# Fold behind the first pool tile, a third quad in the turns, split output weights kept in DRAM

## The chip, the cores and the metric

One Trainium2 chip, one of its cores. The metric is the time of one execution on the device in microseconds, as the median of several runs. Five engines run their own instruction queues: TensorE (PE), VectorE (DVE), ScalarE (ACT), GpSimd (POOL) and SyncE (SP). SP issues nearly all DMA transfers.

## The reference, cut to what matters

One decoder block on 2048 tokens of 1024 features, all float32:

```
z = rmsnorm(x) @ w_in + b_in              # 1024 -> 1536: a, gate, p of 512 each
conv = silu(layernorm(dwconv31(a * sigmoid(gate))))
pool_i = (trailing mean over w_i - p_i) @ w_pool[i], times s_pool   # 4 groups of 128, w = 2, 4, 8, 16
h = x + concat(conv, pool) @ w_out
h = h + (silu(hn @ w_gate) * (hn @ w_up)) @ w_down,  hn = rmsnorm(h)   # hidden width 2816
out = rmsnorm(h)
```

## The kernel before

**Products in float32.** Each operand of a large matmul is split into a high and a low part: ACT rounds it (`split`, L197), DVE subtracts (L198). `mm3` (L206 to L208) then issues three matmuls, high by high, high by low and low by high. A matmul has a 128x128 stationary block (weights) and 512 moving columns (tokens).

**Tiling.** The tokens go in two tiles of 1024 (`a0`, `a1`, `Sup`), each in two blocks of 512. Features lie on partitions. A tile passes the input projection (`in_tile`, with `in_evac` or `pool_evac`), the branches (`conv`, `ln`, `pool`), the output projection (`mix_out`, PSUM tile `px`), the norm (`norm`) and the feed-forward part (`gate_up`). The second tile's projection and branches run beside the first one's later stages.

**The fold.** The pool group's linear map is folded into the output weights: `fold()` splits `w_pool * s_pool`, and then, in four steps, loads 512 KB of `w_out`'s pool rows (`Dense(wop[i])`), splits them, issues 6 matmuls, copies the result and writes it to DRAM as `wf_d`. At the top level its first step stands behind the second GLU tile; the other four stand between the last two pairs of input tiles.

**Output weights.** `mix_out(b)` runs eight weight tiles for each block b, and is called for b = 0 and b = 1. `Ahead` makes each tile (two loads of 256 KB into staging, a split) two tiles ahead of its use, in both blocks and for both token tiles: 32 times in all.

**Quads.** Gate and up projections use one level of Strassen's scheme: a quad (L859 on) is 256 output features by 1024 tokens by 1024 inputs, in seven products of 12 matmuls instead of eight. Products 1 to 7 use token factors `t[1]` to `t[7]`, made by `put_t` from the four quarters of the normed h, and weight factors a to d made by `first` (a), `sums` (d, then four additions in place, L895 to L898), `mid` (b) and `last` (c). Quads with an even number are gates, the others ups. A quad's results lie in one PSUM tile of two halves (`acc`); the intermediate `ch` is one half of the PSUM tile `chain`, quads taking turns. Product 1 is copied from `acc` to `ch` (L971), and then product 2 adds to `acc`.

**The turn.** `turn(s, gu)` leads from the output projection to the quads. It steps three generators by hand: `m1` (`mix_out(1)`), `nm` (the norms; row sums L319, spread of the factors through a matmul with ones L349, scaling of eight columns L641) and `gu` (`gate_up`). In the transition `gate_up` runs quads 0 and 1 product by product while `put_t` makes the factors; the others follow in a loop, each quad's first product beside the end of the one before.

**What sets the order.** The order in which the kernel's text issues instructions gives priorities. A scheduler lays them out at compile time with its own estimate of times, per engine: the first ready one in the text's order goes first, so later work is drawn forward into gaps it foresees. On the chip each engine's order, SP's DMA queue too, is fixed. SBUF is given out by two lists of slots, `arena` (17 slots, staging and float32 data) and `arena_r` (36 slots, split data): `take` picks the free slot that was given back longest ago, in the text's order, and the new user waits for the old one's readers.

Of the kernel before, what the change touches and what calls it, by code (L numbers as in the profile page):

```python
# [104 lines left out]
def block_kernel(ctx: ExitStack, tc: tile.TileContext, x, xt, wi, wo, wop, wg, wu, wd, wp, par, out):  # L105
# [41 lines left out]
    p_d = dram("p_d", NCI, PH + TT)  # L147
    y_d = [dram(f"y_d{s}", KD, TT) for s in range(NS)]
    wf_d = dr.tile([P, KD * CC], F32, name="wf_d", bufs=1)
    h_d = [dram(f"h_d{s}", NQ, 2 * TT) for s in range(NS)]  # L150
# [59 lines left out]
    class Dense:  # L210


        def __init__(self, src, halves=False, parts=None, pairs=None):
            self.place = (lambda k: (k % pairs, k // pairs)) if pairs else (lambda k: (k // 2, k % 2))
            n = src.shape[1] // 2 if parts is None else T
            st = Buf(arena, 2 * n)
            v = st.ap.rearrange("p (a n) -> p a n", a=2)
            self.w = W(2, n)
            w = self.w.v
            self.per = n // P  # L220
            if halves:
                self.part = lambda a: (nc.sync.dma_start(v[:, a], src[:, a * n : (a + 1) * n]), split(w[:, 0, a], w[:, 1, a], v[:, a]))
                self.st = st
                return
            else:
                if parts is None:
                    nc.sync.dma_start(v, src.rearrange("p (a n) -> p a n", a=2))
                else:
                    parts(v)
                split(w[:, 0], w[:, 1], v)  # L230
            st.free()

# [122 lines left out]
    class Sup:  # L355
# [235 lines left out]
        def mix_weights(self):  # L591
            def maker(m):
                def parts(v):
                    nc.sync.dma_start(v[:, 0], wo[m])
                    nc.sync.dma_start(v[:, 1], wf_d[:, m * CC : (m + 1) * CC])

                return lambda: Dense(None, parts=parts)

            self.mw = Ahead([maker(m) for m in range(KD)] * 2, 2)
            self.mw.prime(2)  # L600

        def mix_out(self, b):
            self.hr = Rms(NT // 2)
            if b == 0:
                self.h = []
            ws = self.mw
            ks = list(range(NCI, KD)) + list(range(NCI))
            for q in range(NQ):
# [25 lines left out]
        def norm(self, b, hr, bank=None):  # L634

            hr.rows(1.0 / D, RMS_EPS, bank)
            yield
            hr.spread()
            for k in range(KD):
                v = self.h[k // 2].v[:, k % 2, b]  # L640
                stt(out=v, in0=v, scalar=col(O_GF, k), in1=hr.rb[:, 0], op0=ALU.mult, op1=ALU.mult)  # L641
                if k % 2:
                    yield
# [3 lines left out]
        def put_t(self, p, half, blk, *terms):  # L647

            self.t[p] = R(f"t{p}")
            for j in range(2):  # L650
# [7 lines left out]
        def gate_up(self):  # L658
# [13 lines left out]
            q0.load()  # L672
            q1.load()
            yield
            yield from self.put_t(1, *B11)
            yield from self.put_t(2, *B21)
            q0.first()
            q1.first()
            q0.sums()
            q0.mid()  # L680
            q1.sums()
            q0.begin()
            q1.begin()
            self.bank = q0.acc[:, 1]
            yield
            q0.product(1)
            yield
            q0.product(2)
            yield
            q1.product(1)  # L690
            q1.product(2)
            q1.mid()
            yield
            yield from self.put_t(5, *B11, B12, B11)
# [12 lines left out]
            run(self.put_t(4, *B21, B21, B11))  # L707
            quads[2].first()
            q0.product(4)
# [5 lines left out]
            quads[2].sums()  # L715
            quads[2].product(1)
            q1.product(4)
# [4 lines left out]
            for n in range(2, len(quads) - 2):  # L722
                cur, nxt, far = quads[n : n + 3]
                cur.product(2)
                cur.last()
                if far and n > 1:
                    far.load()
# [131 lines left out]
    class Quad:  # L859
# [6 lines left out]
        at = None  # L866
        acc = None

        def __init__(self, sup, n):
# [64 lines left out]
        def result(self, a, b, acc, extra=None):  # L934
# [6 lines left out]
            else:  # L941
                tt(out=dst, in0=acc, in1=dst, op=ALU.mult)

        def begin(self):
            if self.acc is None:
                self.acc = ps2("quad")

        def product(self, p):
            if p == 1:
                self.begin()  # L950
                self.open()
            b1, b5, ch = self.acc[:, 0], self.acc[:, 1], self.ch
# [17 lines left out]
            if p == 1:  # L970
                nc.scalar.copy(ch, b1)  # L971
            elif p == 2:
                self.result(0, 0, b1)
            elif p == 6:
# [125 lines left out]
    for i in range(2, NCI):  # L1100
        pa = a0.in_tile(in0.get(), "pa")
        step(cv, 5)
        step(fo)
        pg = a0.in_tile(in0.get(), "pg")
        a0.in_evac(i, pa, pg)
        step(cv, 4)
        step(fo)
    run(fo)
    sq1 = a1.squares()
    for i in range(NCI):  # L1110
        pp = a0.in_tile(in0.get(), "pp")
        a0.pool_evac(i, pp)
        step(cv, 4)
        if i < 3:
# [33 lines left out]
    def turn(s, gu):  # L1148
# [5 lines left out]
        step(m1)  # L1154
        step(nm)
        step(m1, 2)
        step(gu)
        for n, _ in enumerate(m1):
            if n < 2:
                step(nm, 2)  # L1160
            elif n == 2:
                step(nm)
            elif n < 5:
                step(gu, 2)
            elif n == 6:
                step(gu)
# [92 lines left out]
```

## Time and profile before

| | |
|---|---|
| Three runs | 1859.98, 1857.26, 1859.78 us; median 1859.78 |
| The profiled execution | 1857.97 us, span 1856.2 us |
| PE busy | 97%, 7803 matmuls |
| DVE busy | 75% |
| ACT busy | 38% |
| DMA, all queues | 289 MB, 156 GB/s over the span |
| Mean granted clock of PE | 0.988 |

The stages of the first token tile, from the timeline of PE: input projection to 155 us, with the fold's matmuls between 70 and 109; the second tile's input projection and the first one's convolution to 319; output projection to 410; transition to some 450; quads and the down projection after that. The second token tile's output projection runs from 1082 to 1171, its transition to some 1213.

A busy PE is not PE at its peak, since its matmuls overlap and their ends are modelled; the count of matmuls in a stretch says more. A line like L198 is that of a helper, so its groups hold many tiles.

### The profile page before, as it was taken

Reading aid. Unit: us, or ns where it says so; the run is one execution under the profiler, and the core shown is the slowest. Engines: PE = TensorE matmul, PEld = TensorE weight load, DVE = VectorE, ACT = ScalarE, POOL = GpSimd, SP = SyncE. Lnnn points to the kernel's source line nnn. Section 1 sums busy time; section 2 is a strip of 40 time slices with the busy share of each in tenths; the row PEclk is TensorE's granted clock in tenths of the full one; section 3 lists DMA queues with packets and bytes.
Section 4 is the critical chain, followed back from the end, with each engine's and each line's share of the span. In section 5 each row is a group of like instructions: output and inputs, shape, how many; then the busy total and the mean of one; then the engine's idle time right before and its main releaser. Section 6 shows DMA issues by size and latency. Waiting matters only on the chain.

```text
span 1856.2 us, 19925 instructions
## 1 busy us (share of the span) xinstructions
PE 1799.8 (97%) x7803; PEld 1460.2 (79%) x7803; DVE 1389.7 (75%) x1607; ACT 698.9 (38%) x900; POOL 54.1 (3%) x41
## 2 busy tenths in 40 slices
PE   8999999998999999999999999899999999999996
PEld 6887887876888888887778878678888888787885
DVE  5979997388899987999987546866555554868645
ACT  6255125234333333344444323333333333635420
POOL 0013200000000000000000000000000000000000
PEclk9999999999999999999999999999999999999998
DMA  8263224622343222337578763144423232667532
GB/s 301 75 210 125 69 92 159 223 84 91 131 166 113 97 97 98 130 109 275 207 271 303 260 207 114 68 175 156 151 87 146 86 108 91 231 245 272 215 103 91
DMA packets 84511, 289.15 MB, mean 156 GB/s; under 512 B 7616, under 2 KB 11840, under 8 KB 71104
## 3 DMA queue, kind: packets, MB, share of 16 engines
q1 hardware_dynamic: 83120, 285.69, 43.4%
q10 hardware_dynamic: 1296, 2.19, 0.3%
q8 instruction: 61, 1.00, 0.2%
q14 instruction: 34, 0.28, 0.0%
HBM read 201.77 MB, written 86.08 MB: 155 GB/s over the span
## 4 chain that ended last, share of the span: by engine, by line
PE 77%; DVE 10%; DMA 6%; ACT 3%; issue 2%; SPq 0%; POOL 0%; POOLq 0%; DVEq 0%; ACTq 0%
PE quad L206 10%; PE quad L207 10%; PE quad L208 10%; PE chain L206 8%; PE chain L207 8%; PE chain L208 8%; DVE arena_r L198 4%; PE px L206 2%; PE px L207 2%; PE px L208 2%; PE pd L206 2%; PE pd L208 2%; PE pd L207 2%; DVE arena L496 2%; ACT arena_r L197 1%
## 5 line engine op out<-in xcount | busy, mean ns | idle before, releaser
L197 ACT CAST arena_r<-arena 128x1024 fp32r<-128x1024 f32 (+2 forms) x431 | 414.6, 976 | 715.1 <-PE quad L207 199.1
L198 DVE TENSOR_TENSOR arena_r<-arena,arena_r 128x1024 fp32r<-128x1024 f32 (+2 forms) x431 | 479.9, 1129 | 181.1 <-ACT arena_r L197 176.7
L206 PE MATMUL quad<-arena_r 128*128 128x512 f32 x960 | 375.7, 392 | 4.3 <-ACT chain L971 1.4
L207 PE MATMUL quad<-arena_r 128*128 128x512 f32 x960 | 375.0, 391 | 1.3 <-DVE arena_r L198 1.3
L208 PE MATMUL quad<-arena_r 128*128 128x512 f32 x960 | 374.9, 391 | 0.0
L206 PE MATMUL chain<-arena_r 128*128 128x512 f32 x720 | 290.3, 403 | 12.0 <-ACT chain L971 6.6
L496 DVE SCALAR_TENSOR_TENSOR arena<-arena,par_sb 128x1024 f32<-128x1024 f32 (+1 forms) x240 | 287.5, 1214 | 2.5
L207 PE MATMUL chain<-arena_r 128*128 128x512 f32 x720 | 282.9, 393 | 5.2 <-DVE arena_r L198 5.2
L208 PE MATMUL chain<-arena_r 128*128 128x512 f32 x720 | 283.1, 393 | 0.0
L206 PEld LDWEIGHTS quad<-arena_r 128*128 128x128 f32 x960 | 180.8, 188 | 46.1 <-DVE arena L1010 2.8
L207 PEld LDWEIGHTS quad<-arena_r 128*128 128x128 f32 x960 | 181.0, 189 | 39.4 <-DVE arena_r L198 2.1
L208 PEld LDWEIGHTS quad<-arena_r 128*128 128x128 f32 x960 | 180.9, 188 | 37.8
L206 PEld LDWEIGHTS chain<-arena_r 128*128 128x128 f32 x720 | 136.2, 189 | 58.8 <-ACT chain L971 22.0
L207 PEld LDWEIGHTS chain<-arena_r 128*128 128x128 f32 x720 | 136.5, 190 | 33.9 <-DVE arena_r L198 6.7
L208 PEld LDWEIGHTS chain<-arena_r 128*128 128x128 f32 x720 | 136.3, 189 | 29.7
L206 PE MATMUL px<-arena_r 128*128 128x512 f32 x256 | 100.1, 392 | 1.0 <-DVE arena L622 1.0
L208 PE MATMUL px<-arena_r 128*128 128x512 f32 x256 | 99.7, 389 | 0.0
L207 PE MATMUL px<-arena_r 128*128 128x512 f32 x256 | 99.7, 389 | 0.0
L937 DVE TENSOR_TENSOR arena<-quad,arena 128x512 f32<-128x512 f32 x88 | 60.4, 686 | 40.6 <-ACT arena L978 28.8
L206 PE MATMUL pd<-arena_r 128*128 128x512 f32 x192 | 75.0, 391 | 2.7 <-ACT arena_r L197 1.9
L208 PE MATMUL pd<-arena_r 128*128 128x512 f32 x192 | 74.7, 389 | 0.0
L207 PE MATMUL pd<-arena_r 128*128 128x512 f32 x192 | 74.7, 389 | 0.0
(142 smaller groups left out, 2026.2 us busy)
## 6 DMA issues: line engine op xcount, KB each, us to landing
arena<-t_d SPq DMA_DIRECT2D x28, 1024.0 KB, 5.8
arena<-h_d SPq DMA_DIRECT2D x28, 1024.0 KB, 6.1
arena<-in_wu SPq DMA_DIRECT2D x44, 512.0 KB, 4.4
arena<-in_wg SPq DMA_DIRECT2D x44, 512.0 KB, 4.3
h_d<-arena SPq DMA_DIRECT2D x20, 1024.0 KB, 4.5
t_d<-arena SPq DMA_DIRECT2D x16, 1024.0 KB, 4.6
arena<-in_wd SPq DMA_DIRECT2D x32, 512.0 KB, 5.0
arena<-in_x SPq DMA_DIRECT2D x12, 1024.0 KB, 7.1
```

The source lines that it names most:

```text
L197: nc.scalar.copy(hi, y)
L198: tt(out=lo, in0=y, in1=hi.bitcast(F32), op=ALU.subtract)
L206: nc.tensor.matmul(acc, lhsT=w[:, 0, c], rhs=hi, start=start, stop=False, **kw)
L207: nc.tensor.matmul(acc, lhsT=w[:, 0, c], rhs=lo, start=False, stop=False, **kw)
L208: nc.tensor.matmul(acc, lhsT=w[:, 1, c], rhs=hi, start=False, stop=stop, **kw)
L496: stt(out=v, in0=u.ap[:, j : j + n], scalar=w, in1=v, op0=ALU.mult, op1=ALU.add)
L937: tt(out=dst if self.gate else extra, in0=acc, in1=extra, op=ALU.add)
```

## The change

Three edits. The fold's four steps are run at one place, behind the evacuation of the first pool tile. The output weights of the second pass of the first token tile are written to DRAM after their split (`wo_s`, 1 MB each), and the second token tile loads these instead of loading and splitting; in a second pass tiles are made one ahead instead of two. In the transition, weight sums come before the token factors 1 and 2, the row factors are spread into the second half of the third quad's PSUM tile instead of a tile of their own, one product of quad 1 stands ahead of that spread, and the third quad's products 1 and 2 run inside the transition: `ahead` loads its first half once more, and the copy of product 1 goes to SBUF (`kept`) and comes back to `ch` in `resume`.

```
         # Dense.__init__
+            if kept is not None:
+                self.w = W(2, kept.shape[1] // 4)
...
+                nc.sync.dma_start(self.w.ap.bitcast(F32), kept)
+                return
...
                 split(w[:, 0], w[:, 1], v)
+                if keep is not None:
+                    nc.sync.dma_start(keep, self.w.ap.bitcast(F32))
         # mix_weights
+            if self.s:
+                ms = [lambda m=m: Dense(None, kept=wo_s[m]) for m in range(KD)] * 2
+            else:
+                ms = [maker(m, k) for k in (None, wo_s) for m in range(KD)]
+            self.mw = Ahead(ms, 2)
         # mix_out
             ws = self.mw
+            ws.depth = 2 - b
         # norm
-            hr.spread()
+            hr.spread(self.bank2 if b else None)
         # gate_up
             q0.load()
             q1.load()
-            yield
-            yield from self.put_t(1, *B11)
-            yield from self.put_t(2, *B21)
+            for p in (1, 2):
+                self.t[p] = R(f"t{p}")
+            yield
             q0.first()
             q1.first()
+            yield
             q0.sums()
             q0.mid()
             q1.sums()
+            yield
+            yield from self.put_t(1, *B11)
+            yield from self.put_t(2, *B21)
             q0.begin()
             q1.begin()
             self.bank = q0.acc[:, 1]
             yield
             q0.product(1)
+            q2 = quads[2]
+            q2.begin()
+            self.bank2 = q2.acc[:, 1:]
             yield
             q0.product(2)
-            yield
             q1.product(1)
+            yield
             q1.product(2)
             q1.mid()
+            q2.ahead()
             yield
...
             run(self.put_t(4, *B21, B21, B11))
-            quads[2].first()
             q0.product(4)
...
-            quads[2].product(1)
+            quads[2].resume()
             q1.product(4)
...
-                cur.product(2)
+                if n > 2:
+                    cur.product(2)
         # Quad
+        def ahead(self):
+            e = Buf(arena, TT)
+            nc.sync.dma_start(e.ap, self.s1)
+            self.put("a", e.ap.rearrange("p (u n) -> p u n", u=2), 2)
+            e.free()
+            self.kept = Buf(arena, T)
+            self.product(1)
+            self.product(2)
+
+        def resume(self):
+            nc.scalar.copy(self.ch, self.kept.ap)
+            self.kept.free()
+            self.kept = None
+            self.open()
+            self.result(0, 0, self.acc[:, 0])
         # product
             if p == 1:
-                nc.scalar.copy(ch, b1)
+                nc.scalar.copy(ch if self.kept is None else self.kept.ap, b1)
             elif p == 2:
-                self.result(0, 0, b1)
+                if self.kept is None:
+                    self.result(0, 0, b1)
         # top level
         a0.in_evac(i, pa, pg)
         step(cv, 4)
-        step(fo)
-    run(fo)
     sq1 = a1.squares()
     for i in range(NCI):
         pp = a0.in_tile(in0.get(), "pp")
         a0.pool_evac(i, pp)
+        run(fo)
         step(cv, 4)
         # turn
         step(nm)
+        step(gu)
         step(m1, 2)
...
-            elif n < 5:
+            elif n == 3:
+                step(gu)
+            elif n < 6:
                 step(gu, 2)
```

## Rows read from the trace of the kernel before

**Rows 1.** Part 1 of the page: engines, busy us, share of the span, instructions.

```profile
PE 1799.8 (97%) x7803; PEld 1460.2 (79%) x7803; DVE 1389.7 (75%) x1607; ACT 698.9 (38%) x900; POOL 54.1 (3%) x41
```

**Rows 2.** Windows: stretch, its us, busy us (instructions) per engine, clock, DMA share, GB/s.

```profile
402.00:452.00 50.00, 40.65 (x153) 29.80 (x152) 41.85 (x51) 20.60 (x25) 1.01 (x1) 0.90 0.18 64
1164.00:1213.00 49.00, 39.71 (x149) 28.99 (x147) 41.50 (x51) 20.60 (x25) 1.01 (x1) 0.90 0.15 54
...
142.00:166.00 24.00, 20.21 (x79) 15.93 (x80) 23.60 (x26) 21.12 (x56) 11.30 (x4) 0.93 0.35 120
365.00:402.00 37.00, 37.00 (x169) 30.74 (x168) 27.33 (x34) 14.86 (x15) 1.01 (x1) 1.00 0.30 100
...
575.00:600.00 25.00, 25.00 (x110) 20.29 (x109) 24.89 (x29) 7.50 (x11) 0.00 (x0) 1.00 0.39 137
```

**Rows 3.** Timeline of PE: start, us, line, operands, in brackets the wait before, releaser.

```profile
411.13 0.39 PE L208 MATMUL quad<-arena_r 128*128 128x512 f32 x1
413.71 1.05 PE L319 MATMUL quad<-ones,arena 128*128 128x1 f32 x8 [2.20 <-DVE arena L303]
...
416.35 0.63 PE L207 MATMUL quad<-arena_r 128*128 128x512 f32 x1
...
419.46 0.62 PE L349 MATMUL rb<-arena_r,ones_r 128*128 128x512 f32 x2
...
423.53 0.50 PE L206 MATMUL quad<-arena_r 128*128 128x512 f32 x1 [0.72 <-ACT chain L971]
...
439.62 0.63 PE L206 MATMUL chain<-arena_r 128*128 128x512 f32 x1
...
442.30 0.79 PE L206 MATMUL chain<-arena_r 128*128 128x512 f32 x1 [1.20 <-ACT arena L976]
...
445.88 0.63 PE L208 MATMUL chain<-arena_r 128*128 128x512 f32 x1
```

**Rows 4.** Timeline of DVE in the first turn.

```profile
405.04 1.28 DVE L895 TENSOR_TENSOR arena<-arena 128x512 f32<-128x512 f32 x2
...
411.59 0.68 DVE L622 TENSOR_TENSOR arena<-px,arena 128x512 f32<-128x512 f32 x1
...
416.44 1.28 DVE L337 TENSOR_TENSOR arena_r<-ident,rs 128x512 fp32r<-128x512 f32 x2
420.12 1.41 DVE L641 SCALAR_TENSOR_TENSOR arena<-arena,par_sb,rb 128x512 f32<-128x512 f32 x2 [2.40 <-PE rb L349]
...
423.71 1.40 DVE L641 SCALAR_TENSOR_TENSOR arena<-arena,par_sb,rb 128x512 f32<-128x512 f32 x2
...
426.58 0.69 DVE L942 TENSOR_TENSOR arena<-quad,arena 128x512 f32<-128x512 f32 x1 [0.34 <-PE quad L208]
...
435.50 3.48 DVE L198 TENSOR_TENSOR arena_r<-arena,arena_r 128x1024 fp32r<-128x1024 f32 x3
```

**Rows 5.** Waits of PE: who waited for whom, us in total, times, longest.

```profile
PE chain L206 <- ACT arena L976: 3.7, 4, 1.2
...
PE pd L206 <- ACT arena_r L197: 1.9, 1, 1.9
```

**Rows 6.** DMA issues over the whole span: KB each, median us to landing.

```profile
arena<-t_d SPq DMA_DIRECT2D x28, 1024.0 KB, 5.8
...
arena<-in_x SPq DMA_DIRECT2D x12, 1024.0 KB, 7.1
...
wf_d<-arena SPq DMA_DIRECT2D x4, 512.0 KB, 4.9
```

**Rows 7.** Timelines of DVE (first row) and PE ahead of and behind the pool tiles.

```profile
107.62 1.23 DVE L414 TENSOR_TENSOR arena<-pg,arena 128x1024 f32<-128x1024 f32 x1 [4.07 <-PE pg L208]
...
142.89 0.50 PE L206 MATMUL pp<-arena_r 128*128 128x512 f32 x1 [1.31 <-ACT arena_r L197]
...
158.18 2.96 PE L525 MATMUL chain<-arena_r 128*128 128x512 f32 x9 [2.18 <-ACT arena L402]
```

More of the change, by code (lines that the diff above doesn't have):

```diff
@@ L148, in block_kernel @@
     y_d = [dram(f"y_d{s}", KD, TT) for s in range(NS)]
+    wo_s = [dr.tile([P, 4 * T], F32, name=f"wo_s{i}", bufs=1) for i in range(KD)]
     wf_d = dr.tile([P, KD * CC], F32, name="wf_d", bufs=1)
@@ L210, in block_kernel, with __init__ @@
     class Dense:
-        def __init__(self, src, halves=False, parts=None, pairs=None):
+        def __init__(self, src, halves=False, parts=None, pairs=None, keep=None, kept=None):
+            if kept is not None:
+                self.w = W(2, kept.shape[1] // 4)
+                self.per = kept.shape[1] // 4 // P
+                self.place = lambda k: (k // 2, k % 2)
+                nc.sync.dma_start(self.w.ap.bitcast(F32), kept)
+                return
             self.place = (lambda k: (k % pairs, k // pairs)) if pairs else (lambda k: (k // 2, k % 2))
@@ L591, in mix_weights, with maker @@
         def mix_weights(self):
-            def maker(m):
+            def maker(m, k):
                 def parts(v):
@@ L595, in parts @@
                     nc.sync.dma_start(v[:, 1], wf_d[:, m * CC : (m + 1) * CC])
-                return lambda: Dense(None, parts=parts)
-            self.mw = Ahead([maker(m) for m in range(KD)] * 2, 2)
+                return lambda: Dense(None, parts=parts, keep=k and k[m])
+            if self.s:
[3 more added lines that the diff above has]
+            self.mw = Ahead(ms, 2)
             self.mw.prime(2)
@@ L647, in put_t @@
         def put_t(self, p, half, blk, *terms):
-            self.t[p] = R(f"t{p}")
+            if p not in self.t:
+                self.t[p] = R(f"t{p}")
             for j in range(2):
@@ L673, in gate_up @@
             q1.load()
+            for p in (1, 2):
+                self.t[p] = R(f"t{p}")
+            yield
+            q0.first()
+            q1.first()
+            yield
+            q0.sums()
+            q0.mid()
+            q1.sums()
             yield
@@ L676, in gate_up @@
             yield from self.put_t(2, *B21)
[L677 to L681, printed above, removed]
             q0.begin()
@@ L686, in gate_up @@
             q0.product(1)
+            q2 = quads[2]
+            q2.begin()
+            self.bank2 = q2.acc[:, 1:]
             yield
             q0.product(2)
+            q1.product(1)
             yield
-            q1.product(1)
             q1.product(2)
             q1.mid()
+            q2.ahead()
             yield
@@ L723, in gate_up @@
                 cur, nxt, far = quads[n : n + 3]
-                cur.product(2)
+                if n > 2:
+                    cur.product(2)
                 cur.last()
-                if far and n > 1:
+                if far:
                     far.load()
@@ L867, in block_kernel @@
         acc = None
+        kept = None
         def __init__(self, sup, n):
@@ L950, in product @@
                 self.begin()
-                self.open()
+                if self.kept is None:
+                    self.open()
             b1, b5, ch = self.acc[:, 0], self.acc[:, 1], self.ch
@@ L970, in product @@
             if p == 1:
-                nc.scalar.copy(ch, b1)
+                nc.scalar.copy(ch if self.kept is None else self.kept.ap, b1)
             elif p == 2:
-                self.result(0, 0, b1)
+                if self.kept is None:
+                    self.result(0, 0, b1)
             elif p == 6:
@@ L1106, in block_kernel @@
         step(cv, 4)
-        step(fo)
-    run(fo)
     sq1 = a1.squares()
```

## The prediction

> **What bounds the kernel now.** Read the page's part 1 first: TensorE (PE) is busy 1799.8 us of 1856.2 [rows 1]. None of its matmuls goes away here, so a gain can only come from PE's lost time. The table of windows shows where that is. A full stretch holds 110 matmuls in 25 us, a pitch of 0.227 us, so 12 matmuls, one product of a quad, cost 2.72 us. The window 402 to 452 holds 153 instructions, 8 of them the short row sums (1.05 us): 50 - 145 x 0.227 - 1.05 = 16 us are lost there. The second turn, 1164 to 1213, loses the same: 49 - 141 x 0.227 - 1.05 = 16 us. The window 142 to 166 holds 79: 24 - 79 x 0.227 = 6 us lost [rows 2]. The rest is small.
>
> Then the timeline of PE in the first turn [rows 3]. After product 1 of the first quad (q0) PE waits 2.20 us for the last sum of squares, runs q0's product 2 partly at a pitch of 0.43 us (the 0.63 us matmuls: granted clock at 1.2 GHz, after 411.5 to 415 with little for PE to do), spreads the norm at 419.46, and then waits again and again, for 1.20 us at 442.30. From 439.62 to 445.88 another 12 matmuls run at the half clock (12 x 0.2 = 2.4 us). VectorE's (DVE) timeline says why [rows 4]: from 420.12 to 439 it has no gap worth the name (0.34 us). It scales the columns (L641), subtracts (L654) and splits (L198), and PE takes each piece as it comes. So between 420 and 442 the turn is bound by DVE, and PE's missing work is what fills it or doesn't.
>
> **The change part by part.** The sum is made against the profiled execution, 1857.97 us (span 1856.2 and 1.8 around it); the three runs have a median of 1859.78, 1.8 above.
>
> *Weight sums moved up.* Two quads' sums (L895 to L898) lie at 405.04 to 411, right ahead of the last evacuation L622 at 411.59, [rows 4], while PE's last px matmul starts eight quad matmuls (1.8 us) before that of 411.13 [rows 3], at 409.3. The instructions stay the same, about 7 us with the splits d and b; the stretch 365 to 402 has 37 - 27.3 = 9.7 us of DVE idle to take them [rows 2]. But the weight slots come free only as px tiles end, and the splits of t1 and t2 now come behind the sums. Bounds 0 to 1.7 us earlier for the row sums; I take 1.5, so row sums at about 412.2. If the cover fails, L622 stays where it is and nothing is lost.
>
> *Third quad's products 1 and 2 in the turn.* They take 24 matmuls = 5.45 us out of the stretch behind the turn, where PE is full. The order becomes: row sums, q0's product 2, q1's product 1, spread, q1's product 2, third quad's 1 and 2, then product 5. The spread now stands behind 5.45 us of matmuls: 412.2 + 1.3 + 5.45 = 418.95, if the clock stays up, and its diagonals are ready by then (DVE finished them 4.0 us after the row sums began). The norm thus starts at some 419.6, 0.5 us before its 420.12 [rows 3, 4].
>
> Then a new wait. The spread goes to the second half of the third quad's PSUM tile, and its products write the first half. Trace: q1's product 6 writes one half of the tile chain and waits 1.20 us at 442.30 for L976, which copies the other half; such waits come 4 times, 3.7 us [rows 3, 5]. So halves of one tile are kept apart as if they were one. No row shows a read held by a matmul to the other half; I assume that it is held alike. In the order of the program the norm's columns 0 and 1 come before the third quad, columns 2 to 7 behind it. So the next L641 waits until the third quad's product 2 ends: q1's product 2 from 419.6 to 422.3, third quad's product 1 to 425.1, the copy between (0.72 us wait, as ahead of 423.53), product 2 to 428.6. L641 goes at 428.75 instead of 423.71, 5 us late. Queued behind it on DVE are three rounds of L641, L654 and L198 (1.32 + 1.13 + 1.13 = 3.6 us each), and PE's products 5 and 6 wait for each.
>
> DVE can do other things meanwhile. Of the 15.2 us from 423.71 to 438.91, 10.8 are those three rounds; the split of the first t5 half (1.13), the result L942 (about 0.95 with its wait) and one of two c splits (1.13) can come before 428.75, the other c split stays. 428.75 + 10.8 + 1.13 = 440.7 against 438.91: the chain that PE waits for in product 6 ends 1.8 us later, and behind it 5.45 us are gone. Gain 3.7 us a turn. Bounds: reads not held and both slow-clock stretches gone, 5.45 + 0.5 + 2.4 = 8.4 us; reads held and DVE idle meanwhile, 428.75 + 15.2 = 443.95, 5.0 late, a gain of 0.4. I take 3.7 because DVE's rows name the work that is ready. For both turns -7.4.
>
> The Trainium skill's page "PSUM — Partial Sum Buffer" (Summary: rules for kernel authors) advises to read PSUM in a different bank while a matmul runs, and calls each bank a separate memory. By that rule a half, which is one bank, would not hold the other, and the turn would gain 8.4 us. The waits for L976 differ from it: here it is the tile that waits.
>
> The third quad's own load of its first half (512 KB, twice as before) is issued where SyncE's queue is nearly idle, and its split takes a pair of slots that the diagonals hold until the spread; cast and subtract, 2.2 us, end by about 422, just as the product is due. Its extra ScalarE copy at resumption (0.57) lies beside product 3. No cost; if it comes 1 us late, the turn gains 1 us less.
>
> *Split output weights kept.* In the first turn's second pass eight writes of 1 MB go out on SP. DMA is used 30% there at 100 GB/s [rows 2]; they hide. A slot is used again one tile (5.45 us) after its split's write has had more than that; no cost, bounds 0 to 2. In the second turn 16 loads of 1 MB take the place of 32 of 256 KB and 16 splits. px has no PE wait there, so the saved DVE time buys nothing itself. The pass has only one tile ahead: where all slots are taken (I count two tiles) the load starts when the tile two before ends, and must land in 5.45 us. Loads of 1 MB land in 5.8 (the nearest row, also SP, also into SBUF) to 7.1 us [rows 6]: a wait of 0.5 to 1.8 each, I take +1.0 for two. Ahead of px, PE waits 1.89 us for a down weight's cast at 1072.86; its load stands behind loads and splits of output weights, which now need no staging slot. Between 0 and -1.9 [rows 5], taken -1.0.
>
> *Fold.* Its 24 matmuls leave 70 to 109 and come behind the first pool tile; PE's work is the same, so the later pool tiles come when they did. Four splits (1.1 us DVE each) move from a stretch where DVE is full to one where it waits 4.07 us [rows 7]. Against that, four loads and four writes (4.9 us each [rows 6]) now stand on SP's queue, and in staging slots, before the second token tile's x loads. The window 142 to 166 already waits for such slots: the fourth pool tile 1.31 us for its weights, the chain at 158.18 2.18 us [rows 7]. 4 MB more at the 300 GB/s or so of full queues is 13 us; the second tile's diagonals were ready 3.5 us ahead of need, so up to +9.5; if all of that window's loss goes, -6.5. Value +1.5, nearer to the loss because the slots are what the rows name.
>
> Sum: -7.4 + 1.0 - 1.0 + 1.5 = -5.9: 1852.1 from the profiled time, 1853.9 from the median; I say 1853.
>
> **Rivals.** (a) Halves don't hold each other: -16.8 + 1.5, that is 1842.7. For it: the page's rule, and that no row shows a read held. Against: the L976 waits. (b) The turn gives it back: DVE stands idle until 428.6, a gain of 0.4 a turn, +0.7 in all: 1859. For it: an order fixed beforehand need not bring up the c splits; in the trace they stand behind L654 at 435.5. (c) Slower: kept weights come late. Place: second turn, second pass. If each of its tiles gets its slot only two tiles before and loads take 7.1 + 0.2 us, seven waits of 1.85 = 13 us, less 5.9: 1865. It decides from 5.45 + 5.9 / 7 = 6.3 us a load. Against: the DMA queues are half idle there, and most tiles have an older slot.
>
> **How the numbers follow.** Forecast 0.46 (own range 1847 to 1857), (a) 0.14, (b) 0.22, (c) 0.12, and 0.06 for a fold that costs its bound. A measurement can tell 0.2%, 3.7 us. Faster: 0.40 of the forecast, (a), 0.02 of (b): 0.56. Same: the forecast's rest 0.06, most of (b), 0.24. Slower: (c), the fold and 0.02 of (b): 0.20. The range reaches from (a) to (c): 1841 to 1865.
>
> **What would show it.** Right: 24 quad matmuls between q1's product 2 and product 5; L641's third column waiting for a quad matmul; the waits ahead of product 6 still there, later by 2 us; the third quad's product 6 right behind q1's product 3. Wrong: L641 running through (a); PE waits on the kept weights' DMA in px (c); a longer wait ahead of the chain at 158; or a PE order in which the third quad comes behind product 5.

## The result, and the profile after

The changed kernel takes 1879.85 us (median of 4, 1878.72 to 1883.42), the kernel before 1858.72 beside it: ratio 1.0124 [1.0111, 1.0136]. That is slower, and 15 us above the upper end of the range. The profiled execution has a span of 1878.6 us.

Part 1 of the page after, to be laid beside [rows 1]: PE has the same 7803 matmuls, the other engines as many instructions or fewer, and the span is 22 us longer. So the engines lost time and got no more work; only DMA moved more, 307 MB instead of 289.

```profile
PE 1810.4 (96%) x7803; PEld 1464.8 (78%) x7803; DVE 1373.2 (73%) x1591; ACT 683.4 (36%) x886; POOL 42.6 (2%) x41
```

To find where, take each stage's length less 0.227 us per matmul of 512 columns that starts in it (7707 of them in either trace): what PE lost there, to waits and to matmuls at the lower clock. The stages are bounded by the starts of matmuls.

| PE lost, us | to first pool tile | pool tiles | to first px | px to row sums | next 62 us (turn) | up to second px | px to row sums | next 62 us (turn) | to the last matmul |
|---|---|---|---|---|---|---|---|---|---|
| before | 12.1 | 2.5 | 9.2 | 4.7 | 15.5 | 15.0 | 3.6 | 17.3 | 17.1 |
| after | 9.9 | 12.0 | 15.3 | 17.3 | 22.0 | 11.4 | 1.2 | 16.4 | 14.0 |

The pool tiles and what follows them cost 15.6 us; 2.2 had been gained ahead of them, so the first output projection begins 13.4 us later, at 332.1. It costs another 12.6 and the first turn 6.5; the second token tile gains 10. Windows, columns as in [rows 2], one of the kernel before and then those of the kernel after: at 100 to 150 DVE, which in the kernel before is busy 39.77 there, is busy 29.89; in 400 to 450, now mostly the second pass of px, PE has 178 matmuls where 220 fit, and the clock is 0.90.

```profile
100.00:150.00 50.00, 47.96 (x211) 39.09 (x210) 39.77 (x40) 27.40 (x41) 9.77 (x8) 1.00 0.62 211
```

```profile
100.00:150.00 50.00, 41.33 (x169) 32.35 (x168) 29.89 (x27) 24.89 (x29) 4.61 (x6) 0.93 0.73 249
150.00:200.00 50.00, 45.18 (x180) 35.27 (x178) 44.69 (x46) 31.11 (x77) 13.82 (x6) 0.90 0.26 88
...
400.00:450.00 50.00, 45.03 (x178) 35.39 (x178) 29.06 (x38) 14.87 (x19) 1.01 (x1) 0.90 0.48 180
...
1192.00:1242.00 50.00, 42.81 (x169) 32.35 (x168) 37.62 (x44) 21.16 (x26) 1.01 (x1) 0.93 0.22 76
```

PE's timeline after. The longest wait for weights in the pool tiles was 1.31 us, ahead of the fourth, in [rows 7]; now it is 6.53, ahead of the third (96 pp matmuls stand before it). Then come waits for weights in px, where there was none (the four longest are shown), and two in the third quad's product 1, behind the spread.

```profile
137.99 0.79 PE L207 MATMUL pp<-arena_r 128*128 128x512 f32 x1 [6.53 <-ACT arena_r L198]
...
401.16 0.50 PE L207 MATMUL px<-arena_r 128*128 128x512 f32 x1 [3.10 <-ACT arena_r L198]
402.72 0.79 PE L209 MATMUL px<-arena_r 128*128 128x512 f32 x1 [0.83 <-DVE arena_r L199]
417.73 0.50 PE L207 MATMUL px<-arena_r 128*128 128x512 f32 x1 [1.47 <-ACT arena_r L198]
419.47 0.80 PE L207 MATMUL px<-arena_r 128*128 128x512 f32 x1 [1.00 <-ACT arena_r L198]
...
451.37 0.50 PE L207 MATMUL quad<-arena_r 128*128 128x512 f32 x1 [1.88 <-ACT arena_r L198]
454.04 0.79 PE L209 MATMUL quad<-arena_r 128*128 128x512 f32 x1 [1.94 <-DVE arena_r L199]
```

DVE's timeline, one row of the kernel before and then the kernel after (L494 and L503 begin a convolution, here the second one; L655 is L641 of before). DVE waits 7.53 us for the second tile's x, and the second convolution begins 24 us later. It has no wait of its own: in DVE's order it stands behind the splits of x. In both turns the third column (the second L655) waits for a quad matmul, as forecast: 13.0 and 9.5 us behind the first, where 9.2 was forecast and [rows 4] have 3.6.

```profile
120.14 0.81 DVE L494 TENSOR_SCALAR arena<-arena,par_sb 128x1024 f32<-128x1024 f32 x1
```

```profile
127.13 2.48 DVE L203 SCALAR_TENSOR_TENSOR arena_r<-arena,par_sb,arena_r 128x1024 fp32r<-128x1024 f32 x2 [7.53 <-ACT arena_r L202]
...
144.50 0.81 DVE L503 TENSOR_SCALAR arena<-arena,par_sb 128x1024 f32<-128x1024 f32 x1
...
449.72 1.40 DVE L655 SCALAR_TENSOR_TENSOR arena<-arena,par_sb,quad 128x512 f32<-128x512 f32 x2
...
462.68 2.06 DVE L655 SCALAR_TENSOR_TENSOR arena<-arena,par_sb,quad 128x512 f32<-128x512 f32 x3 [5.22 <-PE quad L209]
...
1208.92 1.40 DVE L655 SCALAR_TENSOR_TENSOR arena<-arena,par_sb,quad 128x512 f32<-128x512 f32 x2
...
1218.43 2.06 DVE L655 SCALAR_TENSOR_TENSOR arena<-arena,par_sb,quad 128x512 f32<-128x512 f32 x3 [2.97 <-PE quad L209]
```

SP's queue, before and then after: the fold's loads and the first load of the second tile's x. In the kernel after the fold's last load goes at 107.09, and x, which stands behind it and two of the fold's writes, at 117.98 instead of 90.11.

```profile
65.37 8.00 SPq L227 DMA_DIRECT2D arena<-in_wop  x2
...
90.11 0.33 SPq L380 DMA_DIRECT2D arena<-in_x  x1
```

```profile
73.13 12.79 SPq L234 DMA_DIRECT2D arena<-in_wop  x2
...
107.09 0.33 SPq L234 DMA_DIRECT2D arena<-in_wop  x1
...
117.98 0.91 SPq L389 DMA_DIRECT2D arena<-in_x  x1
```

### The profile page after: what moved, and what is told of

Same layout as the page of the kernel before. It is cut to its first block, busy times and chain, and to the rows that moved or that the text cites. A ratio compares the mean times of both kernels' runs of the same rounds, so it can differ in the third digit from the quotient of the medians.

```text
span 1878.6 us, 19878 instructions
## 1 busy us (share of the span) xinstructions
PE 1810.4 (96%) x7803; PEld 1464.8 (78%) x7803; DVE 1373.2 (73%) x1591; ACT 683.4 (36%) x886; POOL 42.6 (2%) x41
## 4 chain that ended last, share of the span: by engine, by line
PE 83%; DVE 8%; DMA 3%; ACT 2%; issue 1%; POOL 0%; SPq 0%; POOLq 0%; DVEq 0%; ACTq 0%
PE quad L207 11%; PE quad L209 11%; PE quad L208 11%; PE chain L207 9%; PE chain L208 8%; PE chain L209 8%; PE px L207 2%; PE pd L207 2%; PE px L209 2%; PE pd L208 2%; PE pd L209 2%; PE px L208 2%; DVE arena_r L199 2%; PE pa L209 1%; DVE arena L505 1%
## 5 line engine op out<-in xcount | busy, mean ns | idle before, releaser
L198 ACT CAST arena_r<-arena 128x1024 fp32r<-128x1024 f32 (+2 forms) x415 | 397.6, 974 | 638.6 <-PE quad L208 211.0
L199 DVE TENSOR_TENSOR arena_r<-arena,arena_r 128x1024 fp32r<-128x1024 f32 (+2 forms) x415 | 460.2, 1126 | 175.1 <-ACT arena_r L198 167.7
L207 PE MATMUL px<-arena_r 128*128 128x512 f32 x256 | 103.1, 403 | 6.8 <-ACT arena_r L198 5.6
L209 PE MATMUL px<-arena_r 128*128 128x512 f32 x256 | 102.2, 399 | 1.4 <-DVE arena_r L199 1.4
L208 PE MATMUL px<-arena_r 128*128 128x512 f32 x256 | 101.8, 398 | 0.2 <-DVE arena_r L199 0.2
L1021 ACT COPY arena<-chain 128x512 f32<-128x512 f32 x60 | 35.3, 588 | 114.6 <-PE chain L209 114.6
L207 PE MATMUL pd<-arena_r 128*128 128x512 f32 x192 | 74.9, 390 | 0.8 <-DVE arena L843 0.8
L209 PE MATMUL pd<-arena_r 128*128 128x512 f32 x192 | 74.7, 389 | 0.0
```

The source lines that it names most:

```text
L198: nc.scalar.copy(hi, y)
L199: tt(out=lo, in0=y, in1=hi.bitcast(F32), op=ALU.subtract)
L207: nc.tensor.matmul(acc, lhsT=w[:, 0, c], rhs=hi, start=start, stop=False, **kw)
L208: nc.tensor.matmul(acc, lhsT=w[:, 0, c], rhs=lo, start=False, stop=False, **kw)
L209: nc.tensor.matmul(acc, lhsT=w[:, 1, c], rhs=hi, start=False, stop=stop, **kw)
L1021: nc.scalar.copy(self.s.v[:, 1], ch)
```

## The experiments

**Which edit costs.** One edit at a time on the kernel before (`fold_only`, `keep_only`, `depth_only`: the one-ahead second pass), and the change without some of them.

```
# fold_only: before, and behind pool_evac:  run(fo)   (its step(fo) removed elsewhere)
# keep_only: before, with wo_s, keep= and kept= (two tiles ahead)
# depth_only: before, with  ws.depth = 2 - b
# turn_only: after, without the fold's and the kept weights' edits
# after_unfold: after, with the fold's steps where they were
```

> The kernel before with the fold edit alone. Theory 1 (the fold by itself costs what the stages of the changed kernel show: the first output projection begins 13.4 us later there): about +13 us against before, a PE wait of some 6 us ahead of the third pool tile, and nothing changed behind the first output projection's start. Rival (the fold is harmless by itself; the loss comes only with the other edits, through another order of the same work): within 4 us of before.

> The kernel before with the kept output weights alone: eight writes of 1 MB in the first turn's second pass, sixteen loads of 1 MB in the second turn, still two tiles ahead in both passes. Theory A (loads stand behind the writes on SyncE's queue): the first output projection and turn lose 10 us or more of the 19.3 us lost there in the changed kernel. Theory B (what costs is being only one tile ahead): within 3 us of before, with no more than 2 us of PE waits on px weights in the first turn.

> The kernel before with one tile ahead instead of two in the second pass, nothing else. Theory B (one tile ahead is what costs): 10 to 19 us more in the first turn's second pass and as much in the second turn's, +20 us or more in all. Theory A (the kept writes cost): within 4 us of before.

> The changed kernel without the fold edit and without kept weights: third quad, sums moved up, one tile ahead in second passes, all weights split each time. Theory A (kept writes cost): both turns gain as the changed kernel's second turn did, 3.5 us each, so about -7 us against before. Theory B (one tile ahead costs): the gain of 7 is lost in px, +10 us or more against before.

> The changed kernel with the fold back in its old place: kept weights and the turn's edits together. If the kept writes with one tile ahead cost the 12 us more that the first output projection lost in the changed kernel (neither the writes nor one tile ahead did so alone): about 1868, with PE waits of 1 to 3 us on px weights in the first turn's second pass. If that loss came from the late fold (its results reach DRAM later): px as short as with the turn's edits alone, and the second turn 7 us shorter than there: about 1855.

| | median us | ratio to before |
|---|---|---|
| fold_only | 1876.56 | 1.0110 [1.0091, 1.0128] |
| keep_only | 1855.92 | 0.9998 [0.9986, 1.0009] |
| depth_only | 1854.79 | 0.9989 [0.9977, 1.0001] |
| turn_only | 1862.64 | 1.0037 [1.0023, 1.0051] |
| after_unfold | 1851.28 | 0.9978 [0.9968, 0.9987] |

Each against the kernel before beside it: the fold's edit alone costs 20.1 us (1856.49 beside it), more than the 13 expected, and in the changed kernel 25.7 (21.1 slower with it, 4.6 faster without, 1855.87 beside it). Kept weights and the one-ahead pass do nothing alone. The turn's edits alone are 6.1 us slower, where -7 or +10 had been expected; with the kept weights they are 4.6 faster, so beside them kept weights are worth 10.7. Of this 2.7 lie between the first turn and the second px, and 4.8 from there to the end of the second turn. In turn_only the second turn waits 1.88 and 1.96 us for the split weights of the third quad, and its third column comes 12.2 us behind the first; in after_unfold PE's order is another there, those waits are gone, and the column comes 9.5 behind. Why kept weights change that order isn't shown. DVE in the second turn of turn_only (L652 is L641 of before):

```profile
1187.00 1.40 DVE L652 SCALAR_TENSOR_TENSOR arena<-arena,par_sb,quad 128x512 f32<-128x512 f32 x2
...
1199.21 2.07 DVE L652 SCALAR_TENSOR_TENSOR arena<-arena,par_sb,quad 128x512 f32<-128x512 f32 x3 [4.46 <-PE quad L209]
```

**What holds the turn.** `turn_rbcopy` lets the scalings read a copy of the factors in SBUF, `turn_both` also splits the third quad's first half ahead of the row sums.

```
# turn_rbcopy: turn_only, in norm
             hr.spread(self.bank2 if b else None)
+            rb = hr.rb[:, 0]
+            if b:
+                rbc = Buf(arena, T)
+                nc.scalar.copy(rbc.ap, rb)
+                rb = rbc.ap
...             # the scalings (stt) read rb in place of hr.rb[:, 0]
# turn_both: the same, and in gate_up
             q2.begin()
+            q2.early()    # load and split of "a", taken out of ahead(), in other slots
```

> The turn's edits alone (no fold edit, no kept weights), and the spread norm factors are copied once from the third quad's PSUM tile to SBUF by ScalarE; the eight column scalings read the copy. Theory (scalings of columns 2 to 7 are held until the third quad's product 2, because they read the tile that it writes): the hold of 12 us in DVE goes to under 5, each turn gets 4 to 6 us shorter than with the turn's edits alone, about -10 us against that kernel, 1852. Rival (the hold is only the place where DVE would have waited anyway, since product 1 of the third quad comes late): the hold goes, but the turns stay within 1.5 us each of what they were.

> As the one before, and the third quad's a weights are loaded and split ahead of the row sums, in slots that the output projection's y has just given back, in place of slots that the spread's diagonals hold. Theory 1 (held scalings): same as the one before within 2 us. Theory 2 (the late split of the a weights, with PE waits of 1.9 and 2.0 us behind the spread, is a price of its own): 2 to 4 us a turn better than the one before, 1846 or so.

1851.16 us, 0.9979 [0.9969, 0.9988], and 1849.96, 0.9972 [0.9962, 0.9983]: 4.7 and 5.9 us below the kernel before beside them (1855.87). The copy gives 10.9 us, as expected, the early split hardly anything more there. So it is the shared tile that holds the scalings: DVE in the first turn of after_unfold and then of `unfold_copy` (below), the same but for the copy. Columns 2 and 3 go 12.2 us behind 0 and 1, then 4.2. A scaling takes as long from SBUF as from PSUM (1.41 and 1.40 us for two), so what the copy saves is the wait. The trace has that wait as one for a semaphore which PE raises; what PSUM itself would allow no run shows.

```profile
419.77 1.40 DVE L655 SCALAR_TENSOR_TENSOR arena<-arena,par_sb,quad 128x512 f32<-128x512 f32 x2
...
431.98 2.06 DVE L655 SCALAR_TENSOR_TENSOR arena<-arena,par_sb,quad 128x512 f32<-128x512 f32 x3 [4.47 <-PE quad L209]
```

```profile
419.77 1.41 DVE L660 SCALAR_TENSOR_TENSOR arena<-arena,par_sb 128x512 f32<-128x512 f32 x2
...
423.96 1.41 DVE L660 SCALAR_TENSOR_TENSOR arena<-arena,par_sb 128x512 f32<-128x512 f32 x2
```

**Why the fold costs.** First theory: the fold's split weights take slots of the pool tiles' weights.

```
# fold_own_slots: fold_only, and in fold()
-            w = Dense(wop[i])
+            w = Dense(wop[i], where=(range(7 * RU), range(NR)))
```

> The fold edit alone, with the fold's split weights in slots of the first token tile's unused factor region in place of those that input weights rotate through. Theory S (the fold's second split waits for the first pool tile's weights to be used up, its staging slot is given back 8 us late, and with it come the token loads behind it on SyncE's queue): most of the fold's loss goes, within 6 us of before in place of +20. Theory Q (what costs is four loads and four writes more on SyncE's queue ahead of the token loads, wherever the weights lie): the loss stays above 12 us.

1872.05 us, 1.0091 [1.0074, 1.0108]: some 4 us of 20, with intervals that overlap. Of PE's waits from 100 to 165 the first fence has fold_only's for pool weights, 7.5 us. In fold_own_slots that wait is 0.2 or less, and PE waits 5.8 us at the next step in its place, the spread of the second tile's norm (second fence).

```profile
PE pp L206 <- ACT arena_r L197: 7.5, 1, 7.5
```

```profile
PE chain L349 <- DVE arena_r L337: 6.2, 2, 5.8
```

Then two theories for the rest. D: the second convolution takes its buffer behind the fold's staging in the text, so that DVE, the bound of the branches, runs dry. Q: the fold's loads stand on SP's queue ahead of the x loads. Each experiment mends one and leaves the other.

```
# fold_conv_first: fold_only, and in the first pool tile's round
         a0.pool_evac(i, pp)
+        step(cv, 12 if i == 0 else 4)
         run(fo)
-        step(cv, 4)
# fold_behind_x: fold_only, run(fo) moved to the end of that round
         run(a0.pool(i))
+        run(fo)
```

> The kernel before with the fold's steps behind the first pool tile, and twelve steps of the convolution in the text ahead of the fold (instead of four behind it), so that the second convolution takes its buffer and begins before the fold takes any staging slot. The number of convolution steps is the same in all. Theory D (VectorE is starved: with the fold in between, the second convolution gets a buffer that the fold's staging held, and so VectorE, the bound from 50 to 300 us, has nothing to do at 100 to 150): VectorE's busy time from 100 to 150 goes back from 27 to 37 us or more, the output projection starts at 319 to 324 instead of 334, time 1857 to 1863. Theory Q (the fold's loads stand on SyncE's queue ahead of the second tile's x loads): the queue is the same, the output projection starts at 330 or later, time 1872 to 1878.

> The kernel before with the fold's steps at the end of the first pool tile's round: behind the convolution steps, the x loads and squares of the second tile and the first pool, where the second convolution has still not begun. Theory D (VectorE starved, the second convolution's buffer comes behind the fold): still slow, VectorE busy 26 to 31 us from 100 to 150, the output projection starts at 330 or later, time 1870 to 1878. Theory Q (order on SyncE's queue): the x loads stand ahead of the fold's loads, VectorE no longer waits for x, the output projection starts at 319 to 324, time 1857 to 1863.

1868.21, 1.0072 [1.0052, 1.0091], and 1867.70, 1.0065 [1.0050, 1.0079]: each takes some 8 us of the 20, and neither theory is the whole. Windows of fold_only, fold_conv_first and fold_behind_x: with the convolution first, DVE is busy 48 of 50 us (26.7 in fold_only), and the output projection starts at 329.1 (334.2; before 318.7). With the x loads first DVE stays at 27.7, but PE loses only 6.0 us in the pool tiles (12.8). The edit of fold_conv_first moves two things, the convolution's turn at the buffers and its place in the order of the text (it begins at 67 us there, 53 before its time in the kernel before); which of the two DVE lacked these runs don't tell.

```profile
100.00:150.00 50.00, 40.37 (x166) 31.58 (x165) 26.68 (x25) 25.52 (x31) 3.67 (x6) 0.93 0.68 229
```

```profile
100.00:150.00 50.00, 41.24 (x169) 32.48 (x168) 48.19 (x44) 25.59 (x31) 6.77 (x6) 0.93 0.66 223
```

```profile
100.00:150.00 50.00, 47.29 (x197) 37.49 (x196) 27.73 (x28) 23.59 (x29) 3.06 (x6) 0.97 0.62 202
```

Then mends together: `fold_conv_own` is fold_conv_first with the own slots, `after_conv_own` the whole changed kernel with both, `fold_conv_behind_x` has the convolution and the x loads first.

> The kernel before with the fold's steps behind the first pool tile, with both mends: twelve convolution steps in the text ahead of the fold, and slots of its own for the fold's split weights. If the loss has these two causes and no other: VectorE busy 46 us or more from 100 to 150, TensorE loses 3 us or less in the pool tiles (12 in the fold alone), the output projection starts at 321 or before, time 1853 to 1859. If a third cause remains (the fold's loads ahead of the x loads on SyncE's queue): the output projection starts at 325 or later, time 1862 to 1868.

> The changed kernel whole, with the same two mends. If the late fold is also what made its first output projection lose 13 us (weights behind kept writes): that loss goes too, 3 us or less from there to the first row sums, time 1848 to 1854, as with the fold left where it was (1851.3). If the kept weights' writes cost this by themselves: 8 us or more are lost there, time 1859 to 1866.

> The kernel before with twelve convolution steps first, and the fold's steps at the end of the first pool tile's round, behind the second tile's x loads; no slots of its own. If the x loads behind the fold are a cause beside VectorE's: the output projection starts at 318 to 322, time 1855 to 1860. If the slots are the other cause: TensorE still loses 5 us or more in the pool tiles, the output projection starts at 325 or later, time 1862 to 1868.

1868.01, 1.0054 [1.0042, 1.0067]; 1873.09, 1.0081 [1.0067, 1.0095]; 1870.60, 1.0066 [1.0052, 1.0079]. None reaches the time of its first branch: with slots and convolution mended a third cause stays (the second branch of fold_conv_own). SP's queue and waits in fold_conv_own show where. The fold's fourth load waits 16.2 us for a staging slot that the GLU evacuation (L417) uses until then, x follows at 117.28, and the third pool tile comes at 137.29, after a wait of 7.18 us. The kernel before has such a wait too (last fence): a fold load stands 20.3 us for the same evacuation, up to 65.37, but x comes only 25 us behind it. In fold_conv_behind_x it is the fold's own weights that come late, and PE, whose order is fixed, waits 12.0 us for them with the pool tiles queued behind.

```profile
107.87 0.33 SPq L227 DMA_DIRECT2D arena<-in_wop  x1
...
117.28 0.33 SPq L380 DMA_DIRECT2D arena<-in_x  x1
```

```profile
SPq L227 <- DVE arena L417: 16.2, 1, 16.2
```

```profile
137.29 0.80 PE L206 MATMUL pp<-arena_r 128*128 128x512 f32 x1 [7.18 <-ACT arena_r L197]
```

```profile
PE fold L206 <- ACT arena_r L197: 12.0, 3, 9.3
```

```profile
SPq L227 <- DVE arena L417: 23.2, 2, 20.3
```

To tell the queue from the slots, the fold's transfers were taken off SP's queue, then its loads out of the shared staging.

```
# fold_conv_own_queue: fold_conv_own, the fold's four loads and its writes (two halves each)
-  nc.sync.dma_start(...)
+  nc.gpsimd.dma_start(...)
# fold_apart: the same, its loads through a buffer of their own, outside the arena
+    fst = [const.tile([P, TT], F32, name="fst0")]
# fold_stage: fold_conv_own with that buffer, all on nc.sync
```

> fold_conv_own with the fold's four loads and four writes (each in two halves) issued by GpSimd in place of SyncE. If the third cause is SyncE's queue, standing at a fold load that waits for a staging slot: the first x load of the second tile is issued by 97 (90.1 in the kernel before, 117.3 in fold_conv_own), TensorE loses 4 us or less in the pool tiles, the output projection starts at 322 or before, time 1854 to 1860. If it is the staging slots: the x loads wait for the same slots in their own queue, first x load at 105 or later, the output projection at 326 or later, time 1863 to 1870.

> The same with one staging buffer outside the shared slots for the fold's loads, so that neither SyncE's queue nor the shared staging holds them; the results of the fold still take shared slots. If the staging slots are the third cause: first x load by 97, the output projection at 322 or before, time 1854 to 1860, and 5 us or more less than fold_conv_own_queue. If the queue alone was the cause: the same as fold_conv_own_queue. If neither: 1863 to 1870, with the x loads early and TensorE still waiting in the pool tiles.

> fold_conv_own (convolution first, own slots for the fold's split weights) with one staging buffer outside the shared slots for the fold's four loads, all issued by SyncE; the fold's four results still take shared slots. If the rest of the loss is the shared staging (SyncE standing at a fold load that waits for a slot which the GLU evacuation holds): the fold's loads are through by 95, the first x load of the second tile is issued at 105 or before (117.3 in fold_conv_own, 90.1 in the kernel before), TensorE loses 5 us or less in the pool tiles (9.9), the output projection starts at 324 or before, time 1855 to 1862. If it is not: the output projection at 327 or later, time 1865 to 1870.

The first two, 1884.04, 1.0155 [1.0142, 1.0169], and 1883.64, 1.0150 [1.0136, 1.0164], miss all that was expected and don't decide: GpSimd has an order of its own. In its timeline in fold_conv_own_queue a copy for the halo waits 20.79 us for the GLU evacuation, and the fold's last load goes only then. In fold_apart the loads are no longer late (the last goes at 34.9), and it is as slow: the writes of the fold's results stand behind such a copy and go from 130.14 to 160.79 (116.2 to 121.1 in fold_conv_own), and SP waits for one of them to land before the next pool weights have a staging slot (last fence).

```profile
113.25 5.91 POOL L421 COPY u_halo<-arena 128x30 f32<-128x30 f32 x1 [20.79 <-DVE arena L417]
119.10 0.53 POOL L227 DMA_DIRECT2D arena<-in_wop  x1
```

```profile
130.14 0.84 POOL L1033 DMA_DIRECT2D wf_d<-arena  x1
...
160.79 0.75 POOL L1033 DMA_DIRECT2D wf_d<-arena  x1 [6.81 <-issue]
```

```profile
SPq L228 <- DMA wf_d<-arena: 15.4, 1, 15.4
```

fold_stage: 1860.88, 1.0027 [1.0017, 1.0038]: 5.2 us are left of 11.0, and the output projection starts at 323.0. The shared staging is the larger part of the third cause. Two numbers of the expectation miss: x goes at 109.41 (expected by 105), and PE loses 8.6 us in the pool tiles (expected 5 or less), 5.2 of them in a wait ahead of the third, whose weights are issued at 129.98, behind x and the writes of the fold's results.

```profile
77.53 0.33 SPq L228 DMA_DIRECT2D fst<-in_wop  x1
...
109.41 0.33 SPq L382 DMA_DIRECT2D arena<-in_x  x1
```

**The change without what it lost.** after_unfold with the copy, and with the copy and the early split.

> The changed kernel with the fold where it was before, and with ScalarE copying the spread factors of the turn's norm from PSUM to SBUF, the scalings reading the copy. If the scalings held by the third quad's products cost time in both turns also where kept weights are used: 1843 to 1848, the scalings 3.6 us apart in both turns. If the kept weights already hide the hold: 1850 to 1853, no less than without the copy (1851.3).

> The same with the third quad's first half loaded and split ahead of the row sums, in two of the slots of the branches' results. If the products of the third quad still wait for that split (1.9 us twice in the changed kernel's first turn): 1 to 3 us less than with the copy alone, 1841 to 1846. If the split is no longer late: the same as the copy alone.

1844.20 us, 0.9936 [0.9921, 0.9951], and 1838.83, 0.9906 [0.9892, 0.9921]: faster than both kernels, 12 and 17 us below the kernel before beside them (1856.25). The early split, worth little in turn_both, gives 5.4 here, more than expected. From px to the turn's end PE lost 15.0 us in the first turn of the latter (20.2 in the kernel before) and 13.3 in the second (20.9).

## Why the prediction was wrong

**The failed step is the fold's term**, "+1.5, nearer to the loss because the slots are what the rows name", with bounds of -6.5 (for a window whose loss it works out as 6) and +9.5. It measured +20.1 alone and +25.7 in the changed kernel. Three assumptions under it fell:

- "PE's work is the same, so the later pool tiles come when they did." PE's work stayed the same; the third tile's weights came late (a wait of 6.53 us).
- Four DVE splits would move into a stretch where DVE waits. What DVE does from 100 to 150 isn't only these: the second convolution belongs there, and with the fold ahead of it in the text (its buffer too is given out in that order) DVE did 13 us less in that stretch (39.77 to 26.68 busy in fold_only). The branches, which keep DVE busy for most of the time up to 319, ended later; the convolution put first gave 8 us back. [rows 7] show DVE waiting 4.07 us, and not what fills the gaps.
- The upper bound counted bytes (13 us less 3.5 of slack). The loss came from order: SP stands at a fold load that waits for a staging slot, with x and the next weights behind it. Hence the mends don't add up: 8 us for the convolution, some 4 for the slots, 9 for both (11.0 of 20.1 are left), 6 more for the staging. The last 5 are not explained further.

In the changed kernel another 12.6 us were lost from px to the row sums. It takes the moved fold together with the other edits: fold_only loses 6.8 there (4.7 before), after_unfold 1.2, but after and after_conv_own 17.3 and 15.7. That the kept writes are the partner is argued, not shown, as no run has the moved fold and the turn's edits without them: SP stands at these writes (L239, each waiting for its split) for 36.8 us from 318 to 450 in the kernel after, 21.5 in after_unfold, and the next weights' loads are behind. Why the moved fold changes that order so is open; after_conv_own, which starts px 3.5 us sooner than the kernel after, loses it all the same.

```profile
SPq L239 <- DVE arena_r L199: 36.8, 8, 7.0
```

```profile
SPq L239 <- DVE arena_r L199: 21.5, 8, 5.8
```

**The turn's term, -7.4, failed too where it stood alone:** turn_only measured +6.1. The hold had been foreseen, but with DVE at work meanwhile. In turn_only DVE stood idle for 4.95 and 4.46 us ahead of the third column, and in both turns PE waited 1.88 and 1.96 us for the third quad's split.

**The rest, by its steps.**

- *Reads held:* right, shown by the copy. Where the trace had shown only a write waiting for a read [rows 5], a read of one half waits for writes to the other (4.47 us in after_unfold).
- *Third quad, -3.7 a turn:* with the sums, from px to the turn's end, the second turn of the kernel after lost 17.6 against 20.9, -3.3, of which 2.4 stand ahead of the row sums. The first turn of after_unfold lost 21.2 against 20.2, no gain, as rival (b) has it: DVE stood idle there (4.47 us). The other reason is the text's own "if it comes 1 us late": 34 matmuls of the first two quads stand ahead of the row sums (12 in the kernel before), so the third quad's product 1 stood right behind the spread and waited 1.88 and 1.94 us for its split.
- *Sums moved up, 1.5:* low by the stages, though no run has them alone. From px to the row sums 4.7 became 1.2 in after_unfold, 3.6 became 1.2 in the second turn.
- *Kept weights, +1.0 and -1.0:* zero alone, as summed. No px wait came in the second turn, so rival (c) had no price; the wait ahead of px went (up to second px: 15.0 to 11.4). That they are worth 11 us beside the turn's edits was not foreseen.
- *Rival (a)* needed halves that don't hold. Once the hold is taken away, unfold_copy gains 12.1 us; (a) without the fold's term is 16.8. The Trainium skill's page "PSUM — Partial Sum Buffer" (Summary: rules for kernel authors) advises to read in another bank while a matmul runs. In this kernel that was not enough: with both halves in one tile of the program the scalings waited for the matmuls all the same (4.47 us), until the factors left the tile.
- *"The rest is small"* was a misreading: of the 97 us that PE loses in the kernel before, the three windows named make 38.

Without the fold's term the sum was -7.4, and after_unfold measured -4.6 (by its interval -5.9 to -2.4). That this is near is partly luck: the turn's edits were to give -7.4 and the kept weights nothing, and the runs have +6.1 and -10.7.

## What to carry to other kernels

Work moved on one engine also moves its loads in an in-order queue and its turn at the shared buffers: list what stands behind each of its loads, and which later user takes a slot after it, before counting bytes or busy time. Where several such resources are short at once, mending one uncovers the next, and an edit that costs 20 us gave back 8 by one mend, some 4 by another and 9 by both. Factors that are read many times from a PSUM tile which matmuls also write were worth one copy to SBUF here (10.9 us in turn_rbcopy, 7.5 in unfold_copy).

## What was not expected of the hardware

DMA's rate first followed the delay: in fold_conv_own the transfers ran at 72 GB/s from 60 to 120 us (155 in the kernel before), while SP stood waiting, and at 329 from 120 to 150 (165). The burst then had a price of its own: the two loads of pool weights issued in it took 7.6 and 8.1 us to land, where the five such loads of the kernel before from 60 to 160 have a median of 3.7. Windows of the kernel before, then of fold_conv_own:

```profile
60.00:120.00 60.00, 60.00 (x266) 49.67 (x266) 50.22 (x42) 23.73 (x26) 3.60 (x4) 1.00 0.48 155
120.00:150.00 30.00, 27.96 (x123) 22.52 (x122) 29.09 (x31) 17.08 (x28) 9.56 (x7) 1.00 0.47 165
```

```profile
60.00:120.00 60.00, 60.00 (x267) 49.67 (x266) 59.92 (x52) 17.09 (x19) 12.64 (x5) 1.00 0.23 72
120.00:150.00 30.00, 22.51 (x90) 17.72 (x89) 26.91 (x26) 15.08 (x21) 3.61 (x4) 0.89 0.95 329
```

Issuing the fold's transfers from GpSimd made them late, since its few small copies wait for DVE and a load or a write behind them waits too: 28.5 us above the kernel before in fold_conv_own_queue, against 11.0 with SP alone. The Trainium skill's page "Trainium Kernel Development and Optimization" (Quick Reference) says that issuing from several engines only saves issue time; here it changed the order as well, and at a loss.
